# Seven half products per up-projection pair in the last feed-forward phase, and modulation weights two tiles at a time

## The chip, the core and the metric

The kernel runs on one core of a Trainium2 chip, in one launch. The metric is device time in microseconds (us): the median of three runs, beside which one execution was profiled.

## What is computed

Two layers of a decoder trunk for two request groups with the same weights: a prompt of 512 positions and 8 samples of 4 positions, 544 columns in all. Each layer is feed-forward, mixer (latent attention and a state-space branch), feed-forward; each of the three reads a normalised input that is scaled and shifted by a modulation made from a conditioning vector. What matters here:

```python
mod = (jax.nn.silu(c) @ ada_w + ada_b)[:, None, :]          # 1024 -> 9 * 1024
sh1, sc1, g1, shm, scm, gm, sh2, sc2, g2 = jnp.split(mod, 9, axis=-1)
...
h = rms_norm(x, norm_ffn2) * (1.0 + sc2) + sh2
a, b = jnp.split(h @ ffn2_up, 2, axis=-1)                   # 1024 -> 2 * 2816
x = x + 0.5 * g2 * ((jax.nn.silu(a) * b) @ ffn2_down)       # 2816 -> 1024
```

## The kernel before, in words

Activations lie transposed: features on the 128 partitions, the 544 columns in two halves of 272 (`HN`). Every float32 operand is split into a rounded part and a remainder (`hi`, `lo`), and every product of a weight tile with an input tile is three matmuls into one PSUM bank (`mm3`, lines 78 to 80): hi by hi, hi by lo, lo by hi. A weight unit of up to 128x1024 is loaded by SyncE's queue into one of five `raw` buffers (L55), copied to `whi` by ScalarE (L62) and subtracted to `wlo` by VectorE or GpSimd in turn (L65); `whl` has eight tiles, so four units.

`ffn` (one call per layer and half, four in all) goes through 22 pairs of up-projection tiles, `up[m]` and `up[22 + m]`. Each pair is 2 tiles x 8 k x 2 halves x 3 matmuls; `close_gate` then forms silu(a) * b and its `hi` and `lo` in the tile `mid[m]` (L327 to L331). Pairs 0 and 1 run together, column half 0 first (`front`), because the normalised input of half 1 (`norm_h`, L265 to L275) is still being made. When eight `mid` tiles are full, `do_down` multiplies a chunk of 6 or 8 of them with the down weights for all 8 output tiles and adds the result to `x` (`resid`, L290 to L295). The last chunk of the last phase is followed by the norm and the scaling of the output (`close`, `rstd`, `final`, L1488).

Beside this TensorE makes the modulations of later stages: `ada_steps` are 16 generators of which `tick()` advances the first one in the list by a step, at fixed places in the loops. A step is one weight tile of 128x1024 (k = 0 to 7): a load, and four matmuls of 32 stationary columns on strips of 32 rows of one PSUM tile (L153, two instructions each). They run in the first three phases; the last one has none. In the phases of layer 0 half 0 and layer 1 half 0 they are woven with the tables of the state-space branch (`s5_tables`).

The kernel is written in a tile framework: the order of each engine's instructions is set by a scheduler from the order of the code, from dependencies and from free buffers; buffers are given out as tiles are released. Each engine then takes its instructions strictly in that order.

Of the kernel before, what the change touches and what calls it, by code (L numbers as in the profile page):

```python
# [15 lines left out]
P = 128  # L16
D = 1024
# [8 lines left out]
FCH = ((0, 6), (6, 14), (14, 22))  # L26
NMID = 8
# [4 lines left out]
class Net:  # L32
# [113 lines left out]
    def ada_steps(self, l, i):  # L146
# [168 lines left out]
    def ffn(self, l, j, up, down, pool, spill=None):  # L315
        g = self.mod[l, 3 * j + 2] if (l, 3 * j + 2) in self.mod else None
        nc = self.nc
        mid = {}

# [36 lines left out]
        def do_up(ms):  # L356
            ms = list(ms)
            while ms:
                n = 2 if ms[0] == 0 else 1
                ws = []  # L360
                for m in ms[:n]:
                    self.share = l + j > 0 or m >= 8
                    ws.append((self.unit(up[m], D), self.unit(up[NFF + m], D)))
                    mid[m] = pool.tile([P, 2, 2, HN], F32R, tag="mid", name="mid")
                s = start(ws) if self.head else None
                for hf in range(2):
                    if n == 2:
                        def between():
                            if hf:
                                self.tick()  # L370
                            return self.settle()
                        pss = next(s) if s else self.front([u for w in ws for u in w], hf, between)
                        for i in range(n):
# [1287 lines left out]
```

## Time and profile before

| what | value |
|---|---|
| runs | 3056.64, 3065.47, 3057.44 us; median 3057.44 |
| profiled execution | 3048.91 us, its span 3047.1 us |
| mean granted TensorE clock | 0.98 of full speed |
| TensorE matmuls busy | 2888.8 us, 95% |
| VectorE, ScalarE, GpSimd busy | 1578.5, 878.6, 1236.9 us |
| HBM read and written | 452.99 and 61.75 MB |

The runs and the profiled execution are separate executions. "Busy" is the union of instruction times on an engine; TensorE's matmuls overlap (each is shown with 0.29 us, and the next starts 0.13 us after it), so rates are read from starts. A lower-case name such as `ps` or `mid` is a tile; L78 is line 78 of the kernel before.

### The profile page before, as it was taken

Reading aid. Unit: us, or ns where it says so; the run is one execution under the profiler, and the core shown is the slowest. Engines: PE = TensorE matmul, PEld = TensorE weight load, DVE = VectorE, ACT = ScalarE, POOL = GpSimd, SP = SyncE. Lnnn points to the kernel's source line nnn. Section 1 sums busy time; section 2 is a strip of 40 time slices with the busy share of each in tenths; the row PEclk is TensorE's granted clock in tenths of the full one; section 3 lists DMA queues with packets and bytes.
Section 4 is the critical chain, followed back from the end, with each engine's and each line's share of the span. In section 5 each row is a group of like instructions: output and inputs, shape, how many; then the busy total and the mean of one; then the engine's idle time right before and its main releaser. Section 6 shows DMA issues by size and latency. Waiting matters only on the chain.

```text
span 3047.1 us, 61485 instructions
## 1 busy us (share of the span) xinstructions
PE 2888.8 (95%) x24466; PEld 2677.5 (88%) x24466; DVE 1578.5 (52%) x3139; ACT 878.6 (29%) x1652; POOL 1236.9 (41%) x1434
## 2 busy tenths in 40 slices
PE   6999999999888999999999999999999899899998
PEld 5889999999667889989989999999987579899998
DVE  7384346374664464573454443464556534644344
ACT  3112123234342232122232222233344322322222
POOL 8635434481445249711233552236514551312113
PEclk9999999999999999999999999999999999999999
DMA  7596563647658624683225664345575774223221
GB/s 274 180 314 208 166 188 111 208 132 250 207 173 261 216 80 157 208 299 111 91 97 175 184 175 125 99 129 171 173 239 185 228 245 165 76 79 97 90 84 51
DMA packets 285008, 510.37 MB, mean 167 GB/s; under 512 B 73265, under 2 KB 166834, under 8 KB 284722
## 3 DMA queue, kind: packets, MB, share of 16 engines
q1 hardware_dynamic: 261746, 455.52, 47.2%
q0 software_dynamic: 13760, 42.03, 4.4%
q10 hardware_dynamic: 9216, 8.92, 0.9%
q8 instruction: 192, 3.15, 0.4%
q14 instruction: 94, 0.77, 0.1%
HBM read 452.99 MB, written 61.75 MB: 169 GB/s over the span
## 4 chain that ended last, share of the span: by engine, by line
PE 75%; DVE 8%; POOL 7%; issue 5%; DMA 3%; ACT 1%; SPq 0%; another core or an unknown queue 0%; DVEq 0%; ACTq 0%; POOLq 0%
PE ps L78 21%; PE ps L80 20%; PE ps L79 20%; PE ps L153 2%; PE ps L1264 2%; PE ps L1304 1%; PE ps L1136 1%; DVE ht L272 1%; DVE hlo L275 1%; PE ps L1176 1%; PE ps L786 1%; POOL s5a L729 1%; PE ps L785 1%; POOL s5b L730 1%; POOL s5a L731 1%
## 5 line engine op out<-in xcount | busy, mean ns | idle before, releaser
L78 PE MATMUL ps<-hhi,whi 128*128 128x272 f32 x3776 | 1105.9, 296 | 4.4 <-ACT whi L62 2.2
L79 PE MATMUL ps<-hlo,whi 128*128 128x272 f32 x3776 | 1092.8, 290 | 14.4 <-DVE hlo L275 11.7
L80 PE MATMUL ps<-hhi,wlo 128*128 128x272 f32 x3776 | 1096.1, 291 | 2.9 <-POOL wlo L65 1.8
L78 PEld LDWEIGHTS ps<-hhi,whi 128*128 128x128 f32 x3776 | 712.9, 190 | 54.7 <-issue 31.4
L79 PEld LDWEIGHTS ps<-hlo,whi 128*128 128x128 f32 x3776 | 718.1, 190 | 19.4 <-DVE hlo L275 13.4
L80 PEld LDWEIGHTS ps<-hhi,wlo 128*128 128x128 f32 x3776 | 715.9, 190 | 5.1 <-POOL wlo L65 2.1
L62 ACT CAST whi<-raw 128x1024 fp32r<-128x1024 f32 (+1 forms) x400 | 409.7, 1026 | 959.9 <-PE ps L79 584.4
L65 POOL TENSOR_TENSOR wlo<-raw,whi 128x1024 fp32r<-128x1024 f32 (+1 forms) x140 | 332.1, 2372 | 847.5 <-ACT whi L62 839.0
L65 DVE TENSOR_TENSOR wlo<-raw,whi 128x1024 fp32r<-128x1024 f32 (+1 forms) x260 | 322.8, 1242 | 354.7 <-ACT whi L62 332.0
L78 PE MATMUL ps<-mid,whi 128*128 128x272 f32 x1408 | 411.1, 292 | 2.6 <-ACT whi L62 2.6
L80 PE MATMUL ps<-mid,wlo 128*128 128x272 f32 x1408 | 407.0, 289 | 1.0 <-DVE wlo L65 1.0
L79 PE MATMUL ps<-mid,whi 128*128 128x272 f32 x1408 | 405.3, 288 | 0.0
L78 PEld LDWEIGHTS ps<-mid,whi 128*128 128x128 f32 x1408 | 265.1, 188 | 14.1 <-issue 9.9
L80 PEld LDWEIGHTS ps<-mid,wlo 128*128 128x128 f32 x1408 | 265.4, 188 | 1.5 <-DVE wlo L65 1.5
L79 PEld LDWEIGHTS ps<-mid,whi 128*128 128x128 f32 x1408 | 266.0, 189 | 0.2
L331 DVE TENSOR_TENSOR mid<-th,mid 128x272 fp32r<-128x272 f32 x176 | 192.9, 1097 | 88.9 <-ACT mid L330 88.3
L1351 POOL DMA_INDIRECT strm<-in_cacheT,idx x128 | 132.8, 1038 | 176.5 <-PE ps L1268 76.8
L1351 POOL DMA_INDIRECT strm<-in_cache,idx x128 | 128.7, 1006 | 133.2 <-PE ps L1304 77.3
L329 DVE TENSOR_TENSOR th<-th,ps 128x272 f32<-128x272 f32 x176 | 76.6, 436 | 203.1 <-PE ps L80 202.2
L292 DVE SCALAR_TENSOR_TENSOR x<-ps,mod,x 128x272 f32<-128x272 f32 (+1 forms) x224 | 106.7, 478 | 138.4 <-PE ps L80 138.2
L330 ACT CAST mid<-th 128x272 fp32r<-128x272 f32 x176 | 73.1, 416 | 318.9 <-DVE th L329 318.7
L78 PE MATMUL ps<-zhi,whi 128*128 128x272 f32 x512 | 153.2, 299 | 1.4 <-issue 1.2
(356 smaller groups left out, 4263.7 us busy)
## 6 DMA issues: line engine op xcount, KB each, us to landing
raw<-in_up SPq DMA_DIRECT2D x176, 512.0 KB
raw<-in_ada_w SPq DMA_DIRECT2D x144, 512.0 KB
raw<-in_dn SPq DMA_DIRECT2D x64, 512.0 KB
raw<-in_w_in SPq DMA_DIRECT2D x60, 512.0 KB
strm<-in_cacheT SPq DMA_DIRECT2D x128, 160.0 KB
s5WW<-w2scr SPq DMA_DIRECT2D x32, 512.0 KB
raw<-in_w_glu SPq DMA_DIRECT2D x32, 512.0 KB
strm<-in_cache SPq DMA_DIRECT2D x128, 128.0 KB
```

The costliest lines, as they stand in the source:

```text
L62: nc.scalar.copy(hi[:, :n], r[:, :n])
L65: e.tensor_sub(lo[:, :n], r[:, :n], hi[:, :n].bitcast(F32))
L78: nc.tensor.matmul(out, wh[:, s], rh, start=first, stop=False)
L79: nc.tensor.matmul(out, wh[:, s], rl, start=False, stop=False)
L80: nc.tensor.matmul(out, wl[:, s], rh, start=False, stop=last)
L153: nc.tensor.matmul(ps[32 * j:32 * j + 32, :256], self.cs[:, k], r[:, 256 * j:256 * j + 256], start=k == 0, stop=k == KD - 1)
L292: nc.vector.scalar_tensor_tensor(xx, ps[:, :np_], g[:, m, 0:1], xx, ALU.mult, ALU.add)
L329: nc.vector.tensor_mul(th, th, pb[:, :HN])
L330: nc.scalar.copy(mt[:, hf, 0], th)
L331: nc.vector.tensor_sub(mt[:, hf, 1], th, mt[:, hf, 0].bitcast(F32))
L1264: nc.tensor.matmul(po[32 * j:32 * j + 32], ql[:, a, 4 * bg + j].rearrange("p h t -> p (h t)"), X[j][:, P * a:P * a + P], start=a == 0, sto ...
L1351: self.nc.gpsimd.indirect_dma_start(out=out, out_offset=None, in_=src.rearrange("l n p f -> (l n p) f"), in_offset=bass.IndirectOffsetOnAx ...
```

## The change

In the last feed-forward phase (layer 1, second half) pairs 3 to 21 use Strassen's scheme on a 2x2 grid: two up-projection tiles, two halves of k (512 each), two column halves. `halves` loads both tiles and forms three combined weight tiles and a half one from them (A itself, S, B, S4), with subtractions on VectorE and GpSimd. `crossed` forms four combinations of the input's quarters (t3 and t2 during the front of half 1, t1 before pair 2, t4 after it); t4 takes over the place of a quarter that is no longer needed. `seven` issues seven products of 4 k x 3 matmuls, which share three PSUM banks; ScalarE copies partial sums out between them, and the sixth and seventh product of a pair (`ends`) are issued between the first three of the next pair, or within the next down chunk. To make room, this phase has six `mid` tiles, and its down projection is cut into five chunks of 4, 4, 4, 4 and 6 instead of 6, 8, 8.

In all phases a modulation step now loads two weight tiles in one tick and multiplies both in the next. `s5_setup` was divided into a loop over parts with one part, which does the same work.

```diff
 NFF = 22
-FCH = ((0, 6), (6, 14), (14, 22))
-NMID = 8
+FCH = (((0, 6), (6, 14), (14, 22)), ((0, 4), (4, 8), (8, 12), (12, 16), (16, 22)))
+NMID = (8, 6)
...
+    def halves(self, wa, wb):
+        nc = self.nc
+        V, E = nc.vector, nc.gpsimd
+        ra, rb = self.raw(wa, D), self.raw(wb, D)
+        lo, hi = slice(0, HK), slice(HK, D)
+        s = self.sum.tile([P, D], F32, tag="sum", name="sum")
+        A = self.split(ra, D, V)
+        V.tensor_add(s[:, hi], rb[:, lo], rb[:, hi])
+        V.tensor_sub(s[:, lo], s[:, hi], ra[:, lo])
+        E.tensor_sub(rb[:, lo], ra[:, lo], rb[:, lo])
+        S = self.split(s, D, V)
+        E.tensor_sub(ra[:, hi], ra[:, hi], s[:, lo])
+        B = self.split(rb, D, V)
+        h = self.sum.tile([P, HK], F32R, tag="s4h", name="s4h")
+        l = self.sum.tile([P, HK], F32R, tag="s4l", name="s4l")
+        nc.scalar.copy(h, ra[:, hi])
+        nc.vector.tensor_sub(l, ra[:, hi], h.bitcast(F32))
+        return A, S, B, (h, l)
+    def crossed(self, pool):
+        nc, V = self.nc, self.nc.vector
+        b11, b12, b21, b22 = self.h[0, 0], self.h[1, 0], self.h[0, 1], self.h[1, 1]
+        new = lambda pl, tag: tuple(pl.tile([P, 4, HN], F32R, tag=tag, name="hx") for _ in range(2))
+        t3, t2, t1 = (new(pool, "hx") for _ in range(3))
+        d = self.tmp.tile([P, 4, HN], F32, tag="ht", name="hd", bufs=1)
+        def add(x, b, i):
+            V.tensor_add(x, x, b[i][:, ks].bitcast(F32))
+        def sub(x, a, b, i):
+            V.tensor_sub(x, a[i][:, ks].bitcast(F32), b[i][:, ks].bitcast(F32))
+        def parts(t, x, ks):
+            nc.scalar.copy(t[0][:, ks], x)
+            V.tensor_sub(t[1][:, ks], x, t[0][:, ks].bitcast(F32))
+        pairs = [slice(0, 2), slice(2, 4)]
+        for ks in pairs:
+            x = d[:, ks]
+            sub(x, b22, b12, 0)
+            add(x, b22, 1)
+            V.tensor_sub(x, x, b12[1][:, ks].bitcast(F32))
+            parts(t3, x, ks)
+        for ks in pairs:
+            x = d[:, ks]
+            add(x, b11, 0)
+            add(x, b11, 1)
+            parts(t2, x, ks)
+        yield
+        def differ(t, a, b):
+            d = self.tmp.tile([P, 4, HN], F32, tag="ht", name="hd", bufs=1)
+            for k in pairs:
+                x = d[:, k]
+                V.tensor_sub(x, a[0][:, k].bitcast(F32), b[0][:, k].bitcast(F32))
+                V.tensor_add(x, x, a[1][:, k].bitcast(F32))
+                V.tensor_sub(x, x, b[1][:, k].bitcast(F32))
+                parts(t, x, k)
+        differ(t1, b12, b11)
+        yield
+        t4 = new(self.hp, "h")
+        differ(t4, b21, t2)
+        self.hx = t1, t2, t3, t4
+    def prod(self, ps, w, c0, rhs, first):
+        for k in range(4):
+            self.mm3(ps[:, :HN], w, c0 + k * P, P, (rhs[0][:, k], rhs[1][:, k]), first and k == 0, k == 3,
+                     skip_group_check=True)
...
         ps = self.psum()
-        for k in range(KD):
-            r = self.raw(self.t["ada_w"][l, k * P:(k + 1) * P, i * D:(i + 1) * D], D)
-            for j in range(4):
-                nc.tensor.matmul(ps[32 * j:32 * j + 32, :256], self.cs[:, k], r[:, 256 * j:256 * j + 256],
-                                 start=k == 0, stop=k == KD - 1)
-            if k < KD - 1:
+        for k0 in range(0, KD, 2):
+            rs = [self.raw(self.t["ada_w"][l, k * P:(k + 1) * P, i * D:(i + 1) * D], D) for k in (k0, k0 + 1)]
+            yield
+            for k, r in zip((k0, k0 + 1), rs):
+                for j in range(4):
+                    nc.tensor.matmul(ps[32 * j:32 * j + 32, :256], self.cs[:, k], r[:, 256 * j:256 * j + 256],
+                                     start=k == 0, stop=k == KD - 1)
+            if k0 < KD - 2:
                 yield
...
         def close_gate(pa, pb, mt, hf):
+            close_silu(open_silu(pa), pb, mt, hf)
+        def open_silu(pa):
             th = self.tmp.tile([P, HN], F32, tag="th", name="th")
             nc.scalar.activation(th, pa[:, :HN], AF.Tanh, scale=0.5)
             nc.vector.scalar_tensor_tensor(th, th, 1.0, pa[:, :HN], ALU.add, ALU.mult)
+            return th
+        def close_silu(th, pb, mt, hf):
             nc.vector.tensor_mul(th, th, pb[:, :HN])
             nc.scalar.copy(mt[:, hf, 0], th)
             nc.vector.tensor_sub(mt[:, hf, 1], th, mt[:, hf, 0].bitcast(F32))
+        def seven(m, mt):
+            A, S, B, S4 = self.halves(up[m], up[NFF + m])
+            t1, t2, t3, t4 = self.hx
+            V = nc.vector
+            new = lambda tag, **k: self.tmp.tile([P, HN], F32, tag=tag, name="u" + tag, **k)
+            X, Y, Z = (self.psum() for _ in range(3))
+            x, y, z = (p[:, :HN] for p in (X, Y, Z))
+            self.prod(Y, A, 0, self.h[0, 0], True)
+            p1 = new("sq")
+            nc.scalar.copy(p1, y)
+            end(0)
+            self.prod(Y, S, 0, t2, False)
+            q = new(("rr", "na")[m % 2], bufs=1)
+            nc.scalar.copy(q, y)
+            end(1)
+            self.prod(X, A, HK, self.h[0, 1], True)
+            V.tensor_add(p1, x, p1)
+            th = open_silu(p1)
+            self.tick()
+            self.prod(Y, B, 0, t3, False)
+            r = new(("acc0", "acc1")[m % 2], bufs=1)
+            nc.scalar.copy(r, y)
+            self.prod(Z, S, HK, t1, True)
+            V.tensor_add(r, z, r)
+            def third():
+                self.prod(Y, B, HK, t4, False)
+                close_silu(th, Y, mt, 0)
+                self.tick()
+            def fourth():
+                self.prod(Z, S4, 0, self.h[1, 1], False)
+                V.tensor_add(q, z, q)
+                close_silu(open_silu(q), r, mt, 1)
+                self.tick()
+            self.ends = [third, fourth]
+        def end(i):
+            if self.ends:
+                self.ends[i]()
+                if i:
+                    self.ends = None
 
...
                     self.share = l + j > 0 or m >= 8
+                    if m > 2 and cross:
+                        mid[m] = pool.tile([P, 2, 2, HN], F32R, tag="mid", name="mid")
+                        seven(m, mid[m])
+                        continue
                     ws.append((self.unit(up[m], D), self.unit(up[NFF + m], D)))
...
-                        pss = next(s) if s else self.front([u for w in ws for u in w], hf, between)
-                        for i in range(n):
-                            close_gate(pss[2 * i], pss[2 * i + 1], mid[i], hf)
-                        self.tick(2 + hf)
+                if ms[0] == 2 and cross:
+                    next(more)
+                for hf in range(2 if ws else 0):
+                    if n == 1:
+                        gate(ws[0], mid[ms[0]], hf)
+                        self.tick(hf)
+                        if hf and ms[0] == 2 and cross:
+                            next(more, None)
                         continue
-                    for m, w in zip(ms, ws):
-                        gate(w, mid[m], hf)
+                    def between():
                         if hf:
                             self.tick()
+                        return self.settle()
+                    pss = next(s) if s else self.front([u for w in ws for u in w], hf, between)
+                    if hf and cross:
+                        more = self.crossed(hx)
+                        next(more)
+                    for i in range(n):
+                        close_gate(pss[2 * i], pss[2 * i + 1], mid[i], hf)
+                    self.tick(2 + hf)
                 ms = ms[n:]
...
+            for i in range(2 if last else 0):
+                end(i)
             for m in range(KD):
                 ws[m] = self.unit(down[m][:, m0 * P:m1 * P], n * P)
                 one(m, 0)
+                if m == 0:
+                    for i in range(2):
+                        end(i)
                 if m < late:
                     one(m, 1)
...
-                     tc.tile_pool(name=f"ft{l}{half}", bufs=1, reuse_waits="tile") as ft:
+                self.ends = None
+                room = lambda c, name, bufs: c.enter_context(
+                    tc.tile_pool(name=f"{name}{l}{half}", bufs=bufs, reuse_waits="tile"))
+                with ExitStack() as rooms:
+                    cross = l * half
+                    pool, hx = room(rooms, "fm", NMID[cross]), None
+                    if cross:
+                        hx, self.sum = room(rooms, "fx", 6), room(rooms, "fs", 1)
+                    ft = room(rooms, "ft", 1)
                     self.share = True
...
-                        self.ffn(l, 2, t["up2"][l], t["dn2"][l], pool)
+                        self.ffn(l, 2, t["up2"][l], t["dn2"][l], pool, hx)
```

## Rows read from the trace of the kernel before

**Rows 1.** The page: its first line and the busy time of each engine.
```profile
span 3047.1 us, 61485 instructions
...
PE 2888.8 (95%) x24466; PEld 2677.5 (88%) x24466; DVE 1578.5 (52%) x3139; ACT 878.6 (29%) x1652; POOL 1236.9 (41%) x1434
```

**Rows 2.** Stretches: length, busy us (count) by engine, granted clock, DMA share, GB/s.
```profile
2670.00:2718.40 48.40, 48.40 (x386) 48.40 (x385) 22.49 (x29) 13.72 (x25) 9.75 (x5) 1.00 0.26 76
...
1700.00:1750.00 50.00, 50.00 (x429) 44.86 (x422) 27.52 (x50) 10.43 (x14) 27.10 (x29) 1.00 0.59 180
...
1300.00:1350.00 50.00, 47.38 (x377) 40.95 (x378) 37.58 (x67) 12.17 (x21) 7.97 (x3) 0.95 0.95 318
```

**Rows 3.** Timeline, VectorE in the last phase: start us, us, instruction, [idle before].
```profile
2682.17 2.42 DVE L331 TENSOR_TENSOR mid<-th,mid 128x272 fp32r<-128x272 f32 x1 [0.88 <-ACT mid L330]
...
2690.89 1.23 DVE L65 TENSOR_TENSOR wlo<-raw,whi 128x1024 fp32r<-128x1024 f32 x1 [2.61 <-ACT whi L62]
2692.03 0.43 DVE L328 SCALAR_TENSOR_TENSOR th<-th,ps 128x272 f32<-128x272 f32 x1
...
2694.27 2.42 DVE L331 TENSOR_TENSOR mid<-th,mid 128x272 fp32r<-128x272 f32 x1 [0.88 <-ACT mid L330]
...
2758.73 0.50 DVE L292 SCALAR_TENSOR_TENSOR x<-ps,mod,x 128x272 f32<-128x272 f32 x1 [1.61 <-PE ps L80]
```

**Rows 4.** Timeline, GpSimd in the same phase.
```profile
2681.90 2.39 POOL L65 TENSOR_TENSOR wlo<-raw,whi 128x1024 fp32r<-128x1024 f32 x1 [9.72 <-ACT whi L62]
...
2757.51 2.39 POOL L65 TENSOR_TENSOR wlo<-raw,whi 128x1024 fp32r<-128x1024 f32 x1 [7.45 <-ACT whi L62]
```

**Rows 5.** Instructions by line: count, ns min/median/max, first and last start, form.
```profile
L658 DVE TENSOR_TENSOR tX<-tF,tB x32: 676/692/2583, 145.9 to 1356.7; 128x512 f32<-128x512 f32 x32
...
L666 POOL TENSOR_TENSOR tW<-tS,tC x32: 1166/1172/1635, 150.1 to 1802.8; 128x576 f32<-128x576 f32 x32
...
L62 ACT CAST whi<-raw x8: 834/1048/1052, 2677.7 to 2717.1; 128x1024 fp32r<-128x1024 f32 x6, 128x768 fp32r<-128x768 f32 x2
...
L327 ACT ACTIVATE th<-ps x36: 383/391/400, 2655.2 to 2944.8; 128x272 f32<-128x272 f32 x36
```

**Rows 6.** Timeline, VectorE and GpSimd at the start of the last phase.
```profile
2648.31 0.29 DVE L269 TENSOR_TENSOR hlo<-ht,hhi 128x128 fp32r<-128x128 f32 x1
2655.31 1.23 DVE L65 TENSOR_TENSOR wlo<-raw,whi 128x1024 fp32r<-128x1024 f32 x1 [6.72 <-ACT whi L62]
...
2656.87 5.76 POOL L65 TENSOR_TENSOR wlo<-raw,whi 128x1024 fp32r<-128x1024 f32 x2 [27.53 <-ACT whi L62]
```

**Rows 7.** Timeline, VectorE in the tail.
```profile
3019.51 0.50 DVE L292 SCALAR_TENSOR_TENSOR x<-ps,mod,x 128x272 f32<-128x272 f32 x1 [2.52 <-PE ps L80]
...
3027.42 4.15 DVE L1488 SCALAR_TENSOR_TENSOR fo<-x,c_fing,ny 128x272 f32<-128x272 f32 x8
...
3032.06 0.18 DVE L290 TENSOR_TENSOR rs<-ps,mod 128x32 f32<-128x32 f32 x1
```

**Rows 8.** Timeline, TensorE around modulation steps.
```profile
55.16 0.64 PE L153 MATMUL ps<-raw,cs 128*32 128x256 f32 x8
...
1140.95 1.50 PE L153 MATMUL ps<-raw,cs 128*32 128x256 f32 x22
1142.38 0.76 PE L78 MATMUL ps<-hhi,whi 128*128 128x272 f32 x4
...
1678.61 0.29 PE L80 MATMUL ps<-hhi,wlo 128*128 128x272 f32 x1
1678.83 0.64 PE L153 MATMUL ps<-raw,cs 128*32 128x256 f32 x8
1679.39 0.39 PE L78 MATMUL ps<-hhi,whi 128*128 128x272 f32 x1
1679.62 0.29 PE L79 MATMUL ps<-hlo,whi 128*128 128x272 f32 x1
...
1784.27 0.64 PE L153 MATMUL ps<-raw,cs 128*32 128x256 f32 x8
```

More of the change, by code (lines that the diff above doesn't have):

```diff
@@ L74, in mm3 @@
+    def prod(self, ps, w, c0, rhs, first):
+        for k in range(4):
+            self.mm3(ps[:, :HN], w, c0 + k * P, P, (rhs[0][:, k], rhs[1][:, k]), first and k == 0, k == 3,
+                     skip_group_check=True)
+    def mm3(self, out, w, c0, m, rhs, first, last, **more):
         nc = self.nc
@@ L77, in mm3 @@
         s = slice(c0, c0 + m)
-        nc.tensor.matmul(out, wh[:, s], rh, start=first, stop=False)
-        nc.tensor.matmul(out, wh[:, s], rl, start=False, stop=False)
-        nc.tensor.matmul(out, wl[:, s], rh, start=False, stop=last)
+        nc.tensor.matmul(out, wh[:, s], rh, start=first, stop=False, **more)
+        nc.tensor.matmul(out, wh[:, s], rl, start=False, stop=False, **more)
+        nc.tensor.matmul(out, wl[:, s], rh, start=False, stop=last, **more)
     def setup(self):
@@ L318, in ffn @@
         mid = {}
+        cross = hx is not None
+        chunks, room = FCH[cross], NMID[cross]
         def gate(w, mt, hf):
@@ L365, in do_up @@
                 s = start(ws) if self.head else None
[L366 to L371, printed above, removed]
[L372 to L375 removed]
+                if ms[0] == 2 and cross:
[6 more added lines that the diff above has]
+                            next(more, None)
                         continue
[L377 to L378 removed]
+                    def between():
                         if hf:
                             self.tick()
+                        return self.settle()
[6 more added lines that the diff above has]
+                    self.tick(2 + hf)
                 ms = ms[n:]
         def do_down(c, last):
[L384 removed]
+            m0, m1 = chunks[c]
             n = m1 - m0
@@ L409, in ffn @@
         while done < NFF:
-            n = min(NMID - live, NFF - done)
+            n = min(room - live, NFF - done)
             do_up(range(done, done + n))
             done, live = done + n, live + n
-            if c < len(FCH) - 1 and done >= FCH[c][1] and (live == NMID or done == NFF):
+            if c < len(chunks) - 1 and done >= chunks[c][1] and (live == room or done == NFF):
                 do_down(c, None)
-                live -= FCH[c][1] - FCH[c][0]
+                live -= chunks[c][1] - chunks[c][0]
                 c += 1
@@ L458, in norm_tail, with s5_setup, s5_powers @@
             self.nc.sync.dma_start(out=spill[:, m, c], in_=self.x[:, m, c])
-    def s5_setup(self, l, pool):
+    def s5_setup(self, l, pool, parts=((0, 2),)):
+        for part in parts:
+            yield from self.s5_powers(l, pool, *part)
+    def s5_powers(self, l, pool, c0, c1):
         nc, t = self.nc, self.t
@@ L471, in s5_setup @@
         are, aim, dt = new("are"), new("aim"), new("dt")
-        nc.gpsimd.dma_start(out=are, in_=t["s5_re"][:, l])
-        nc.gpsimd.dma_start(out=aim, in_=t["s5_im"][:, l])
-        nc.gpsimd.dma_start(out=dt, in_=t["s5_dt"][:, l])
+        nc.gpsimd.dma_start(out=are, in_=t["s5_re"][:, l, cols])
+        nc.gpsimd.dma_start(out=aim, in_=t["s5_im"][:, l, cols])
+        nc.gpsimd.dma_start(out=dt, in_=t["s5_dt"][:, l, cols])
         MAGIC = 12582912.0
@@ L578, in s5_setup @@
         yield
-        for h in range(2):
+        for h in range(2 if c1 == 2 else 0):
             fp = pool.tile([P, 4, 2, N], F32, tag="s5fp", name="s5fp", bufs=1)
-            cmul(fp[0:N], pw[0:N, 4 * h:4 * h + 4, :, N:W], f[0:N, :, N:W], 4, N, N)
+            cmul(fp[0:N], pw[0:N, 4 * h:4 * h + 4, :, W - N:W], f[0:N, :, W - N:W], 4, N, N)
             nc.gpsimd.dma_start(out=self.fscr[l][4 * h:4 * h + 4].rearrange("n g q -> g n q"),
@@ L1527, in run @@
                 self.fillers, todo = todo[:n], todo[n:]
-                with tc.tile_pool(name=f"fm{l}{half}", bufs=NMID, reuse_waits="tile") as pool, \
-                     tc.tile_pool(name=f"ft{l}{half}", bufs=1, reuse_waits="tile") as ft:
+                self.ends = None
[7 more added lines that the diff above has]
+                    ft = room(rooms, "ft", 1)
                     self.share = True
```

12 lines of the change are left out of this document (7 added, 5 removed).

## The prediction

> **What bounds the kernel now.** I read the page's table of engines first, then stretches, then single instructions. TensorE is busy 2888.8 of a span of 3047.1 us and nothing else comes near [rows 1]. A share says little of one stage, so the next view is busy time by stretch: in an up-projection stretch of the last feed-forward phase TensorE is busy 48.40 of 48.40 us at full clock, VectorE 22.49, ScalarE 13.72, GpSimd 9.75, and DMA takes 0.26; the modulation steps of the earlier phases run beside an equally full TensorE (50.00 of 50.00), but in a stretch like 1300 to 1350 DMA stands at 0.95 and TensorE at 47.38 [rows 2]. So TensorE's instruction stream sets the time at both places of the change, and a matmul taken out is worth its slot as long as the helpers keep up. How near are they? In one pair's period VectorE runs a weight split of 1.23 us, two gates of 0.43 to 0.44 us operations, and one `mid` subtraction that takes 2.42 us although it is no longer than its sisters [rows 3]. It starts at 2682.17, and GpSimd's split runs 2681.90 to 2684.29 [rows 4]: a VectorE operation with two SBUF operands stands until GpSimd's is done. One with an operand in PSUM doesn't: L292 at 2758.73 takes its usual 0.50 us [rows 3] inside GpSimd's 2757.51 to 2759.90 [rows 4]. This decides the forecast.
>
> **Seven products instead of eight: TensorE.** A pair now is 2 tiles x 8 k x 2 halves x 3 = 96 matmuls, and the pairs come every 2694.27 - 2682.17 = 12.10 us [rows 3], so 0.126 us a matmul. Seven products of 4 x 3 are 84, or 10.59 us. Pairs 3 to 21, 19 of them, save 1.51 us each: **-28.7 us**. The down projections keep their 1056 matmuls. Their cut into five chunks adds 16 smaller weight units and 32 more evacuations; a four-tile unit gives TensorE 24 x 0.126 = 3.0 us, while VectorE needs two or three operations of 0.50 us or less per product and a half-size split, under 2.2 us together. I cost that at nothing; the cover is gone only if VectorE enters the chunk late.
>
> **The pair's helpers.** VectorE gets per pair: three splits of 1.23 (3.69), three half-width operations at the 0.69 of a 512-column one (2.07) [rows 5], and nine of 272 columns at 0.44 (two mid subtractions, three additions, four gate steps; 3.96): 9.7 us. Back to back an operation costs 0.09 less (1.14 from 2690.89 to 2692.03 for one of 1.23 [rows 3]): 8.4. GpSimd does two 512-column subtractions; 576 columns take 1.17 [rows 5] and half of 2.39 [rows 4] is 1.20, so 2.4 us, and 11 of VectorE's 15 operations have both inputs in SBUF and stand meanwhile. VectorE's demand is thus between 8.4 and 9.7 + 2.4 = 12.1 us against TensorE's 10.59: from below it to level with today's pair. I take the middle with the lock mostly felt, 10.9, which costs 0.3 x 19 = **+6 us** (ends 0 and 1.5 x 19 = 28.7). ScalarE needs three casts of 1.05, half a one, and seven of 0.39 to 0.42, 6.5 us, so it is covered, but the second product writes the bank whose first result it copies: it has one product (12 x 0.126 = 1.5 us) for a copy near 0.39 [rows 5] that may queue behind a cast.
>
> [...]
>
> **The crossed sums at the start.** Before the first such pair VectorE forms four combinations of the input: 30 operations of 544 columns, at 0.69 x 544/512 = 0.73, or 0.65 back to back. Fourteen (9.1 us) can start when the last `hlo` ends at 2648.6 and last to 2657.7. Today VectorE starts pair 2's split at 2655.31, with GpSimd on the next two from 2656.87 [rows 6]. Now four gate operations (1.4) and that split (1.2) come behind the sums, to 2660.3 at best, against 2656.5: 3.8 us, and part of GpSimd's 2.4 on top, say 5. The other sixteen (10.4 us), pair 2's gates and pair 3's halves must fit in pair 2's 12.1 us and pair 3's first products; I find VectorE 2 to 3 us late there. Together **+8 us** (3 if the scheduler fits them in, 14 if nothing more than half of 30 x 0.73 = 21.9 is hidden; below nothing is excluded, since no old work leaves this stretch).
>
> **The tail.** After the half-0 result of the last m (its VectorE step follows at 3019.51) TensorE has four products of eight tiles, 3.0 us each, and VectorE fills that time with the norm and the eight final scalings of half 0, 3027.42 to 3031.6; the last residual starts at 3032.06 [rows 7]. With six tiles they take 2.3 us each: 3 us less cover, of which only the earlier norm sum gives 0.7 back: **+2 us** (0 to 3).
>
> **Modulation steps, two tiles at a time.** The loads are the same and come a tick earlier than the matmuls; the count of ticks stays 8. What changes is how often TensorE leaves the 128x128 work for four strips of 32 columns. From L80 at 1678.61 to L79 at 1679.62 is 1.01 us with one step between, where two slots are 0.25: 0.76 us a step, and from the step's start to the next matmul 0.56. Eleven matmuls in a row (22 instructions, three rounds over the strips) take 1.43 [rows 8]: a further round adds (1.43 - 0.56)/2 = 0.43. Two steps together cost 0.76 + 0.43 = 1.19 instead of 1.52: 0.33 a merger. Between 55.16 and 1784.27 I count 111 stretches of one step [rows 8] and 6 longer ones besides the opening one, 118 in all, for 128 steps; in pairs there are at most 64, so 54 fewer: 18 us. Some ten mergers lie where DMA is the limit [rows 2] and give little: **-15 us** (ends 0, if the scheduler pulls the two steps apart, and -18).
> [...]
> Held against this: two of the five `raw` buffers wait for a tick, so weights are fetched less far ahead. A 512 KB unit feeds TensorE for 6 us and the split tiles hold two pairs, so I cost it at nothing; without that cover each late unit would cost its landing.
>
> **Sum.** -28.7 + 6 + 8 + 2 - 15 = -28 us. The profiled execution took 3048.9 us (its span and 1.8 around it), 8.5 below the median of the runs, 3057.4. So 3021 profiled and **3029 us** in the runs. What a measurement of this kernel can tell from no change is about 0.3%, 9 us.
>
> **Rivals.**
> - *All hidden.* VectorE stays under TensorE (8.4 us a pair), the sums cost 3: -28.7 + 3 + 2 - 18 = -42, 3015 us. For it: VectorE was busy under half the time [rows 2], and down chunks let it catch up. Against: the 2.42 us wait. Chance 0.17.
> - *The pairs of steps don't run together.* If TensorE takes up other work between them: -13, 3045 us. For it: the order is the scheduler's; against: both loads land long before. Chance 0.10.
> - *VectorE level with today's pair.* 12.1 us a pair: +8 + 2 - 15 = -5, 3052 us, which is no change. For it: the lock, and a queue that is taken in order. Against: four of the operations read PSUM. Chance 0.13.
> - *Slower: VectorE becomes the bound.* To 12.1 us comes a wait in VectorE's queue for ScalarE's cast of 1.05 us ahead of a split, because one operation that waits holds all behind it: 13.2, +1.1 x 19 = 21, +8 + 2 - 15 = +16, 3073 us. It decides from a pair time of 12.1 + (9 + 5)/19 = 12.8 us. For it: every sum of halves is a chain over VectorE, GpSimd and ScalarE; against: it runs a pair ahead. Chance 0.07.
> - *Forecast*, -15 to -41 about 3029: chance 0.53.
>
> Faster: 0.53 + 0.17 + 0.10 = 0.80; within 0.3%: 0.13; slower: 0.07. The range leaves out the slower case, half of the level one and the far end of the first: 3010 to 3052. The forecast's own is 3016 to 3042.
>
> **What would show it.** Per step: pairs 3 to 21 some 10.9 us apart instead of 12.10, with TensorE's waits on VectorE or ScalarE; near 12 the lock has won. GpSimd's 512-column subtractions near 1.2 us, and VectorE operations stretched over them. A TensorE gap of some 5 us before pair 2, and another in pair 3 or 4. Modulation stretches of 16 instructions, some 0.98 us to the next matmul, half as many as now. A last residual some 2 us later against the end of half 0. It would be wrong if VectorE waits for ScalarE inside the pair, if the split tiles (six of eight used by one pair) make ScalarE wait past the next pair's start, or if late weights open gaps in the earlier phases.

## Result, and the profile after

The changed kernel took 3015.09 us (median of four runs, 3012.52 to 3017.05), the kernel before 3057.04 beside it: ratio 0.9861, interval [0.984, 0.9882], 42 us faster. 3029 had been predicted, with 3010 to 3052 as the range.

The profiled executions differ by less, 3047.1 against 3013.2 us of span (-33.9), because the one of before lay 8.1 us under the median beside it and the one of after at its median. The mixers, which the change doesn't touch, were also 5.4 us longer in the profile of after; outside them the span falls by 39.3 us, from 1869.3 to 1830.0. The page of the changed kernel, its first line and TensorE's:

```profile
span 3013.2 us, 61535 instructions
...
PE 2847.7 (95%) x24238; PEld 2657.3 (88%) x24238; DVE 1705.2 (57%) x3393; ACT 940.3 (31%) x1771; POOL 1254.7 (42%) x1461
```

Beside [rows 1], VectorE has 127 us more to do and TensorE 41 less; TensorE's share of the span stays at 95%. Where that comes from is read by stretch (length, busy us and count of each engine, granted clock, DMA share, GB/s):

```profile
140.00:160.00 20.00, 7.49 (x50) 6.37 (x49) 14.37 (x15) 2.48 (x5) 13.93 (x14) 0.69 0.79 245
...
1700.00:1750.00 50.00, 50.00 (x436) 46.02 (x436) 22.87 (x45) 11.55 (x16) 23.74 (x25) 1.00 0.62 194
...
2650.00:2700.00 50.00, 47.29 (x373) 46.80 (x373) 48.42 (x79) 24.62 (x47) 13.16 (x8) 1.00 0.27 78
...
2700.00:2767.00 67.00, 67.00 (x535) 67.00 (x534) 53.34 (x98) 30.51 (x54) 17.88 (x12) 1.00 0.32 97
```

The last row is one cycle of the new last phase, four pairs and a down chunk: TensorE never stands, and VectorE has 13.7 us to spare. At the phase's start (2650 to 2700) VectorE is full and TensorE loses 2.7 us. At 140 us, far from the products, TensorE is busy 7.49 of 20 us at 0.69 of its clock, where the kernel before has

```profile
140.00:160.00 20.00, 15.27 (x109) 13.11 (x108) 9.64 (x14) 1.20 (x4) 9.53 (x11) 0.83 0.83 248
```

This is the other side of the change, below. TensorE's timeline of the changed kernel (start, duration, instruction, [idle before <- what ended it]):

```profile
151.51 0.59 PE L154 MATMUL ps<-hhi,whi 128*128 128x272 f32 x1 [8.62 <-ACT whi L63]
...
156.23 0.60 PE L156 MATMUL ps<-hhi,wlo 128*128 128x272 f32 x1 [3.90 <-DVE wlo L66]
...
1671.14 1.07 PE L231 MATMUL ps<-raw,cs 128*32 128x256 f32 x16
1672.14 0.39 PE L154 MATMUL ps<-hhi,whi 128*128 128x272 f32 x1
...
2621.51 0.70 PE L325 MATMUL ps<-lsq,ones 128*128 128x272 f32 x2 [2.83 <-DVE lsq L324]
...
2646.70 0.39 PE L154 MATMUL ps<-hhi,whi 128*128 128x272 f32 x1 [0.99 <-ACT whi L63]
...
2665.12 0.39 PE L154 MATMUL ps<-hx,whi 128*128 128x272 f32 x1 [1.78 <-ACT hx L111]
...
2676.12 0.39 PE L156 MATMUL ps<-hx,wlo 128*128 128x272 f32 x1 [0.92 <-DVE wlo L66]
...
2742.87 0.29 PE L154 MATMUL ps<-hhi,s4h 128*128 128x272 f32 x1
...
2753.45 0.29 PE L154 MATMUL ps<-hhi,s4h 128*128 128x272 f32 x1
...
3000.47 0.73 PE L325 MATMUL ps<-lsq,ones 128*128 128x272 f32 x2 [4.36 <-DVE lsq L324]
```

The product with `s4h` comes once a pair, but in three of its four places in a cycle the next one is nearer or farther, because the scheduler moves it against the other products and the down chunk. The two shown have 84 matmuls between them, all of products, and are 2753.45 - 2742.87 = 10.58 us apart, with no wait. The same product of the next cycle starts 66.40 us later (2733.81 to 2800.21) for 4 x 84 + 192 = 528 matmuls, 0.126 us each, so nothing is added in the rest of the cycle either. A stretch of two steps has 16 instructions and takes 1.00 us; with the opening one there are 67 stretches instead of 120, 53 fewer. From the norm's sum at 2621.51 to the end the last phase takes 391.7 us, 23.5 less than before. The first and the last sum of that phase in the kernel before:

```profile
2631.89 0.70 PE L247 MATMUL ps<-lsq,ones 128*128 128x272 f32 x2 [2.83 <-DVE lsq L246]
...
3034.10 0.73 PE L247 MATMUL ps<-lsq,ones 128*128 128x272 f32 x2 [2.11 <-DVE lsq L246]
```

Stage lengths from the profiles of all kernels follow (us, each from the last sum of squares ahead of a stage to the first one behind it, the last phase to the end of the span). The experiments were made in three series (B, C, D), each on one chip and beside runs of the kernel before; series B has the kernel before as a profile of its own.

| kernel | first ffn, layer 0 | second ffn, layer 0 | first ffn, layer 1 | mixers | last phase |
|---|---|---|---|---|---|
| before | 481.1 | 429.4 | 420.0 | 588.9, 588.9 | 415.2 |
| after | 476.1 | 422.7 | 415.9 | 595.0, 588.2 | 391.7 |
| B: e0_before | 479.5 | 430.7 | 420.0 | 551.3, 553.0 | 415.3 |
| B: e1_products | 481.5 | 432.1 | 419.9 | 553.7, 551.4 | 392.5 |
| B: e2_steps | 478.2 | 430.4 | 415.9 | 551.2, 554.5 | 413.5 |
| B: e6_chunks | 483.0 | 431.8 | 419.9 | 553.6, 550.9 | 416.1 |
| C: e10_after | 478.0 | 427.2 | 415.8 | 596.4, 593.5 | 394.1 |
| C: e11_raw6 | 473.0 | 418.8 | 415.8 | 594.0, 596.8 | 391.8 |
| C: e12_steps_raw6 | 473.2 | 419.9 | 415.8 | 593.8, 598.1 | 415.2 |
| C: e7_no_sums | 476.6 | 423.1 | 415.8 | 595.2, 590.6 | 388.6 |
| D: e3_no_gpsimd | 477.3 | 426.1 | 415.8 | 587.7, 587.8 | 389.8 |
| D: e4_vector3 | 474.8 | 424.8 | 415.7 | 593.2, 588.1 | 395.2 |
| D: e5_vector6 | 476.6 | 424.6 | 415.7 | 594.0, 589.3 | 424.3 |
| D: e15_raw6_no_gpsimd | 474.8 | 424.4 | 415.8 | 594.3, 592.0 | 390.5 |

A part of the scatter in the last column is TensorE's clock: over the first 30 us of the phase 0.89 of it is granted in e10_after, e11_raw6 and e15, 0.94 in before, e0_before, after, e1_products, e3 and e7, 1.00 in e2_steps and e6_chunks. A difference of 0.05 to 0.06 over 30 us is 1.5 to 1.8 us.

### The profile page after: what moved, and what is told of

The parts are those of the page before. It is cut to its first block, busy times and chain, and to the rows that moved or that the text cites. A ratio compares the mean times of both kernels' runs of the same rounds, so it can differ in the third digit from the quotient of the medians.

```text
span 3013.2 us, 61535 instructions
## 1 busy us (share of the span) xinstructions
PE 2847.7 (95%) x24238; PEld 2657.3 (88%) x24238; DVE 1705.2 (57%) x3393; ACT 940.3 (31%) x1771; POOL 1254.7 (42%) x1461
## 4 chain that ended last, share of the span: by engine, by line
PE 74%; DVE 9%; POOL 7%; issue 4%; DMA 3%; ACT 1%; another core or an unknown queue 1%; SPq 0%; DVEq 0%; ACTq 0%; POOLq 0%
PE ps L154 21%; PE ps L156 20%; PE ps L155 20%; PE ps L1290 1%; PE ps L231 1%; PE ps L1418 1%; PE ps L1458 1%; PE ps L1330 1%; DVE ht L350 1%; POOL s5a L883 1%; PE ps L940 1%; PE ps L939 1%; DMA raw<-in_dn 1%; DVE hlo L353 1%; DMA raw<-in_up 1%
## 5 line engine op out<-in xcount | busy, mean ns | idle before, releaser
L154 PE MATMUL ps<-hhi,whi 128*128 128x272 f32 x3320 | 969.9, 296 | 14.4 <-ACT whi L63 11.8
L155 PE MATMUL ps<-hlo,whi 128*128 128x272 f32 x3320 | 962.5, 291 | 14.4 <-DVE hlo L353 11.7
L156 PE MATMUL ps<-hhi,wlo 128*128 128x272 f32 x3320 | 963.7, 292 | 7.1 <-DVE wlo L66 4.1
L63 ACT CAST whi<-raw 128x1024 fp32r<-128x1024 f32 (+2 forms) x416 | 412.9, 994 | 904.3 <-PE ps L155 443.9
L154 PEld LDWEIGHTS ps<-hhi,whi 128*128 128x128 f32 x3320 | 627.4, 190 | 47.4 <-issue 21.6
L155 PEld LDWEIGHTS ps<-hlo,whi 128*128 128x128 f32 x3320 | 633.4, 191 | 19.2 <-DVE hlo L353 13.2
L156 PEld LDWEIGHTS ps<-hhi,wlo 128*128 128x128 f32 x3320 | 630.4, 190 | 10.1 <-DVE wlo L66 5.1
L66 POOL TENSOR_TENSOR wlo<-raw,whi 128x1024 fp32r<-128x1024 f32 (+2 forms) x129 | 290.6, 2253 | 671.7 <-ACT whi L63 603.7
L66 DVE TENSOR_TENSOR wlo<-raw,whi 128x1024 fp32r<-128x1024 f32 (+2 forms) x287 | 358.4, 1249 | 338.2 <-ACT whi L63 316.2
L370 DVE SCALAR_TENSOR_TENSOR x<-ps,mod,x 128x272 f32<-128x272 f32 (+1 forms) x256 | 121.6, 477 | 106.5 <-PE ps L156 106.3
L155 PE MATMUL ps<-zlo,whi 128*128 128x272 f32 x512 | 149.1, 291 | 2.8 <-issue 2.6
```

Of the source, the lines that this page charges most:

```text
L63: nc.scalar.copy(hi[:, :n], r[:, :n])
L66: e.tensor_sub(lo[:, :n], r[:, :n], hi[:, :n].bitcast(F32))
L154: nc.tensor.matmul(out, wh[:, s], rh, start=first, stop=False, **more)
L155: nc.tensor.matmul(out, wh[:, s], rl, start=False, stop=False, **more)
L156: nc.tensor.matmul(out, wl[:, s], rh, start=False, stop=last, **more)
L370: nc.vector.scalar_tensor_tensor(xx, ps[:, :np_], g[:, m, 0:1], xx, ALU.mult, ALU.add)
```

## The experiments

**The two halves of the change, each alone.** A copy of the kernel before says what the comparison can tell; the other kernels have the products with the old steps, the steps without the products, and the smaller chunks without either.

> The kernel before once more, to see how far two executions and two profiles of the same program differ. The change brought 42 us in the medians of the runs but only 33.9 us between the two profiled spans (3047.1 and 3013.2), and the mixer of layer 0 looked 6.1 us longer after. If the first profile of before was merely a quick execution: ratio 1.000 within 0.3%, a profiled execution near 3056 us, and the missing 8 us spread over the two mixers, which the change does not touch. If the spans are typical instead, a profiled execution near 3049 again, and the 8 us is something that the change does when it is not profiled.

Measured: 2975.49 us, ratio 1.0001 [0.9988, 1.0014]. The profiled execution took 2975.26, the median of its runs. The chip is another one, on which the same kernel takes 82 us less, so this doesn't say whether the first profile of before was a quick one. But outside the mixers the two spans agree, 1869.2 us here and 1869.3 there.

e1_products keeps `ada_steps` of before in the changed kernel:

```diff
-        for k0 in range(0, KD, 2):
-            rs = [self.raw(..., D) for k in (k0, k0 + 1)]
+        for k in range(KD):
+            r = self.raw(self.t["ada_w"][l, k * P:(k + 1) * P, i * D:(i + 1) * D], D)
...
```

> The seven products alone, with modulation steps of one tile as before. Theory now: the helpers are nearly hidden, and the last phase gains 12 x 19 x 0.126 = 28.7 us less 3 us of waits at its start and 2 us in the tail, so 23 to 24 us: 3033 us where before takes 3057, ratio 0.992. Rival, the sum of the forecast: the helpers cost 16 us, so 13 us gained, 3044 us, ratio 0.996, and the steps must then bring 29 us.

Measured: 2954.81, ratio 0.9931 [0.9916, 0.9945], -20.4 us. Its last phase is 22.8 us shorter than that of the copy.

e2_steps is the reverse edit, made to the kernel before.

> The modulation steps in pairs alone, in the kernel before. Theory: 53 stretches of steps fewer at 0.33 us are 17 us, less some lost to loads near 150 us: 3040 to 3042 us, ratio 0.995. Rival: the steps bring 25 us or more (3032 us or less), because a load that comes a tick earlier also takes waits out of TensorE. Rival: they bring under 8 us, and the remainder of the 42 us came with the products.

Measured: 2965.68, ratio 0.9966 [0.9954, 0.9978], -9.6 us in the medians (10 by the ratio). The phase in which TensorE hardly waits for anything else (first of layer 1, 0.5 us of waits) gave 420.0 - 415.9 = 4.1 us for 12 fewer stretches, 0.34 a merger, against 0.33 forecast. The first phase gave only 1.3 against the copy, though it loses the most stretches (24 of 53). The four kernels with single steps take 479.5 to 483.0 us there, so one pair of profiles says little; but its timeline shows waits for weights that the copy doesn't have,

```profile
152.08 0.60 PE L78 MATMUL ps<-hhi,whi 128*128 128x272 f32 x1 [8.62 <-ACT whi L62]
...
156.64 0.59 PE L80 MATMUL ps<-hhi,wlo 128*128 128x272 f32 x1 [3.75 <-DVE wlo L65]
```

the same two as in the changed kernel. The copy has four smaller ones near there: between 120 and 180 us TensorE waits 12.4 us here and 7.8 in the copy. Its waits in the whole phase are 24.0 us against 17.6 in the copy, and 11.9 against 9.2 in the second.

e6_chunks cuts the down projection of the last phase into five, in the kernel before:

```diff
-FCH = ((0, 6), (6, 14), (14, 22))
-NMID = 8
+FCH = (((0, 6), (6, 14), (14, 22)), ((0, 4), (4, 8), (8, 12), (12, 16), (16, 22)))
+NMID = (8, 6)
```

> The kernel before with six mid tiles and five down chunks (4, 4, 4, 4, 6) in the last phase, without the products. Theory: the matmuls are the same and the 16 further units and 32 evacuations are hidden, so only the tail counts: with six tiles in the last chunk 3 us less of TensorE's work covers the norm and scaling of half 0, of which 0.7 to 1 comes back: +2 us, 3059 us, ratio 1.0007. Rival: every further chunk border costs TensorE a wait of its own, +1 to 3 us each, 3062 to 3066 us.

Measured: 2979.81, ratio 1.0017 [1.0006, 1.0029]. The wait before the last norm sum grows by 2.3, to that of the changed kernel, 4.36 us, where the copy waits 2.10 (TensorE's timeline of e6_chunks):

```profile
2965.11 1.28 PE L247 MATMUL ps<-lsq,ones 128*128 128x272 f32 x2 [4.36 <-DVE lsq L246]
```

So the tail's 2.3 us come from the chunks and their six tiles alone. The last phase is 416.1 us against 415.3, only 0.8 longer, because in its first 30 us the copy had the lower clock and got through 13 matmuls fewer, some 1.6 us (e0_before, then e6_chunks):

```profile
2558.23:2588.23 30.00, 27.75 (x199) 26.90 (x200) 20.89 (x47) 10.48 (x22) 4.99 (x2) 0.94 0.08 22
```

```profile
2562.34:2592.34 30.00, 27.75 (x212) 26.91 (x213) 22.31 (x48) 10.87 (x23) 5.76 (x2) 1.00 0.12 41
```

The runs differ by 4.6 us, with an interval from 1.8 to 8.6 that holds the tail's 2.3; where the rest lies stays open.

**The whole change again, and the raw buffers.** The waits at 152 us had one suspect: a pair of steps holds two of the five `raw` buffers for a tick. e11 and e12 give the pool a sixth.

```diff
-        self.rawp = pool("rawp", 5)
+        self.rawp = pool("rawp", 6)
```

> The whole change, on the same chip as the three kernels below. Alone, the products were worth 20.4 us and the paired steps 10.2 us of 2975 on one chip, while the whole change was worth 42 of 3057 on another. If the parts add up, the ratio is near 0.990 (some 30 us); if the first comparison holds wherever the kernel runs, 0.986 (some 41 us). The last feed-forward phase should be 391 to 393 us from its norm's sum to the end of the span, either way.

Measured: 3024.95 against 3059.89, ratio 0.9875 [0.9855, 0.9896], -35 us; the last phase is 394.1 us, 1 over what was expected. The product of the ratios of the two halves is 0.9897, at the upper edge of this interval and outside that of the first comparison, though it is itself uncertain by some 0.002. Whether the parts do a little more together, or gain a little more on these chips, is not settled.

> The whole change with six raw buffers instead of five. Theory: two of the five buffers held by a pair of steps make the weights late, and the sixth lets a load start earlier: TensorE's waits for a split near 152 to 157 us (8.6 and 3.8 us) and near 1260 us (7.5) shrink to 3 to 4 each, and the time is 6 to 10 us below that of the whole change. Rival: in those stretches the DMA engines are full, the bytes land no earlier, and the time is the same within 2 us.

Measured: 3018.37, ratio 0.9865 [0.9847, 0.9883]; 6.6 us below e10_after, with intervals that overlap. SyncE's queue shows what the buffer changes. First the changed kernel, then e11_raw6:

```profile
121.94 3.17 SPq L56 DMA_DIRECT2D raw<-in_ada_w  x2
125.21 1.25 SPq L56 DMA_DIRECT2D raw<-in_up  x1
140.69 0.65 SPq L782 DMA_DIRECT2D tF<-fscr  x1
...
145.26 0.38 SPq L56 DMA_DIRECT2D raw<-in_up  x1
```

```profile
121.17 1.28 SPq L56 DMA_DIRECT2D raw<-in_ada_w  x3
124.09 0.80 SPq L56 DMA_DIRECT2D raw<-in_up  x2
140.54 0.66 SPq L782 DMA_DIRECT2D tF<-fscr  x1
```

With five buffers one up-projection tile is left for 145.26, behind eight loads of tables in the same queue, the first of which waits 14.2 us for its source to be written; with six it goes out at 124.09 with its sister. TensorE in the same 20 us of e11_raw6:

```profile
140.00:160.00 20.00, 13.92 (x119) 12.04 (x118) 14.33 (x17) 2.16 (x5) 13.02 (x13) 0.91 0.80 259
```

13.92 us busy instead of 7.49, at a DMA share of 0.80 against 0.79: it was a late issue, and not full DMA engines, that held this weight. Not all of it comes back: e11_raw6 then waits 4.72 us at 157 (the next weights), and between 120 and 180 us 9.1 in all, where the changed kernel waits 12.5. The two phases of layer 0 are 473.0 and 418.8 us, against 474.8 to 478.0 and 422.7 to 427.2 in the six profiles of the paired steps with the products and five buffers.

> The kernel before with the paired steps alone and six raw buffers. With five, 10.2 us were gained of some 16 that the fewer stretches give. Theory of the held buffers: 15 to 18 us below the kernel before. Rival (DMA full): 10, as with five buffers.

Measured: 3045.40, ratio 0.9956 [0.9939, 0.9973], -14.5 us, near the theory's lower figure, but the interval (8 to 19 us) holds the rival's 10 as well: the runs alone don't decide here. The three phases with steps gained 7.9 + 9.5 + 4.2 = 21.6 us against the first profile of before. Its mixers are 14 us longer than there, but mixers of kernels that run the same paired steps go from 587.7 to 598.1, so a part of the gain is hidden in that scatter.

**The sums of the input.** Here `crossed` makes nothing, and plain quarters go into the products, so the up-projection is another one (the edit also removes the body of `crossed`):

```diff
...
-        differ(t4, b21, t2)
+        t1, t2, t3, t4 = b12, b11, b22, b21
         self.hx = t1, t2, t3, t4
```

> The whole change without the crossed sums of the input: plain quarters of the input stand in the place of the sums in four of the seven products, so the up-projection of the last phase is another one. It prices the sums: the forecast put them at 8 us (5 before the second pair, the rest in the third or fourth); the rival, that the scheduler fits most of them in, at 3. TensorE's waits ahead of the second to fourth pair (together some 4 us in the profile after) should vanish: 3 to 4 us below the whole change by the rival, 8 by the forecast.

Measured: 3017.79, ratio 0.986 [0.9835, 0.9884]. Its last phase is 388.6 us against 394.1, 391.7 and 391.8 in the three profiles with the sums (e10_after, after, e11_raw6), so they cost 3 to 5.5 us; the 3.1 against after are at the same clock in the first 30 us. Its stretch at the start has TensorE full and VectorE at 39.15:

```profile
2650.00:2700.00 50.00, 50.00 (x399) 50.00 (x398) 39.15 (x61) 23.55 (x45) 13.38 (x9) 1.00 0.31 94
```

**GpSimd beside VectorE, and VectorE's cover.** Three kernels: the two GpSimd subtractions given to VectorE, and three or six additions a pair that nobody needs.

```diff
-        V, E = nc.vector, nc.gpsimd
+        V, E = nc.vector, nc.vector
```

> The whole change with the pair's two GpSimd subtractions done by VectorE. VectorE gets 2 x 0.69 = 1.4 us more a pair and is no longer held up by GpSimd there. Theory (VectorE has cover, 53 to 54 us busy of 67 in a cycle of four pairs and a down chunk): the pairs stay 10.6 us apart and the last phase stays at 391 to 394 us. Rival, VectorE bounds the pair with the lock's cost on top (the forecast's 6 us): the last phase gets some 6 us shorter if the lock was dearer than the work, or up to 1.4 x 19 = 27 longer if the work is.

Measured: 3014.30, ratio 0.9865 [0.9847, 0.9882]; the last phase is 389.8 us. Groups by line of two cycles (2700 to 2833), busy us and mean ns, first of the changed kernel:

```profile
L66 DVE TENSOR_TENSOR wlo<-raw,whi 128x1024 fp32r<-128x1024 f32 x16 | 23.5, 1467 | 1.7 <-ACT whi L63 1.7
L66 DVE TENSOR_TENSOR wlo<-sum,whi 128x1024 fp32r<-128x1024 f32 x8 | 11.8, 1474 | 6.2 <-ACT whi L63 6.2
L84 DVE TENSOR_TENSOR sum<-sum,raw 128x512 f32<-128x512 f32 x8 | 9.3, 1166 | 0.1
...
L85 POOL TENSOR_TENSOR raw<-raw 128x512 f32<-128x512 f32 x8 | 13.7, 1706 | 29.1 <-DVE sum L83 17.9 <-DVE rs L368 6.8 <-PE ps L155 4.4
...
L87 POOL TENSOR_TENSOR raw<-raw,sum 128x512 f32<-128x512 f32 x8 | 10.6, 1329 | 34.6 <-DVE wlo L66 34.6
```

and of e3_no_gpsimd:

```profile
L66 DVE TENSOR_TENSOR wlo<-raw,whi 128x1024 fp32r<-128x1024 f32 x16 | 19.5, 1221 | 2.4 <-ACT whi L63 2.4
L66 DVE TENSOR_TENSOR wlo<-sum,whi 128x1024 fp32r<-128x1024 f32 x8 | 9.8, 1222 | 4.9 <-ACT whi L63 4.9
L85 DVE TENSOR_TENSOR raw<-raw 128x512 f32<-128x512 f32 x8 | 6.6, 821 | 0.0
L84 DVE TENSOR_TENSOR sum<-sum,raw 128x512 f32<-128x512 f32 x8 | 5.5, 686 | 0.1
L87 DVE TENSOR_TENSOR raw<-raw,sum 128x512 f32<-128x512 f32 x8 | 5.5, 684 | 0.1
```

Beside GpSimd's two subtractions the three splits of a pair take 0.25 us more on average (1467 and 1474 ns against 1221 and 1222) and `L84` 0.48 (1166 against 686): 1.2 us of VectorE's time a pair, out of the 3.0 us that GpSimd's two take. VectorE does them itself in 1.5. So VectorE is as busy either way (106.5 us of these 133 in after, 107.8 here), TensorE is full in both, and over the cycle this cost the path nothing.

At the phase's start it is different. The last phase is 1.9 us shorter than in after, with the same clock in its first 30 us, and of the waits at 2646.70, 2665.12 and 2676.12 in the changed kernel, 3.7 us together, one of 0.75 is left:

```profile
2643.38 0.39 PE L156 MATMUL ps<-hhi,wlo 128*128 128x272 f32 x1 [0.75 <-DVE wlo L66]
```

The kernel before has one of 0.74 in the same place, and so has e15 below, which also keeps GpSimd out of the pairs; with GpSimd these waits are 1.6 to 3.7 us (e11, e1, e10 and after). Two waits on the norm ahead of them are 1.1 longer in e3, which leaves the 1.9. So the price of the crossed sums is paid where GpSimd's subtractions come on top of them, while VectorE has no free time (48.42 of 50 us above). Whether because VectorE's operations get longer beside them or because GpSimd's 1.3 to 2.7 us stand in a pair's chain, these kernels don't separate.

For the dose, `halves` ends with

```diff
+        for _ in range(3):
+            more = self.sum.tile([P, HK], F32, tag="more", name="more")
+            V.tensor_add(more, s[:, lo], s[:, hi])
         return A, S, B, (h, l)
```

> The whole change with three more 512-column VectorE additions a pair, whose result nobody reads: 3 x 0.69 = 2.1 us a pair, 39 us in 19 pairs. VectorE's free time is some 13 us in a cycle of four pairs and a chunk, 3.3 a pair. Theory (free time of the whole cycle counts): hidden, the last phase 391 to 396 us. Rival (what counts is the pair alone, because TensorE can't run ahead of the splits): VectorE at 9.7 to 10.5 plus 2.1 is over 10.59 and the last phase is 20 to 39 us longer.

> As the one above with six additions: 4.1 us a pair. Theory (whole cycle): 0.8 us a pair more than VectorE's free time, the last phase 10 to 25 us longer. Rival (the pair alone): 59 to 78 us longer.

Measured: three additions, 3020.23, ratio 0.9887 [0.9861, 0.9912], last phase 395.2 us; six, 3050.15, ratio 0.9974 [0.9957, 0.999], last phase 424.3. The cycle in e4_vector3, then in e5_vector6:

```profile
2767.00:2834.00 67.00, 67.00 (x535) 67.00 (x534) 61.85 (x110) 30.43 (x53) 19.30 (x12) 1.00 0.31 96
```

```profile
2700.00:2767.00 67.00, 63.83 (x495) 63.10 (x495) 65.37 (x111) 26.80 (x47) 17.65 (x11) 0.98 0.30 95
```

The first three go into VectorE's free time (53 to 54 us busy become 62, TensorE stays full), at 1 to 4 us for the phase; the next three don't. The theory that the whole cycle's free time counts holds for the place of the bend. Its price for six was too low (10 to 25 us against 33). The trace says where the 33 lie: TensorE waits 28.0 us in the phase, 9.7 in after, and it is granted less of its clock, 0.95 against 0.98: behind its waits of 2.76 us (to 2697.72) and 3.31 us (to 2984.96) matmuls start 0.23 us apart for 4.0 and 3.3 us, where they otherwise start 0.126 apart. The whole phase of after, then of e5_vector6:

```profile
2621.51:3013.20 391.69, 369.93 (x2908) 367.84 (x2908) 316.82 (x580) 166.25 (x297) 106.39 (x77) 0.98 0.27 83
```

```profile
2623.76:3048.10 424.34, 384.01 (x2908) 377.53 (x2908) 393.55 (x694) 164.02 (x297) 118.46 (x77) 0.95 0.25 77
```

The waits are 18 us more, and the clock is worth some 13 by estimate: 0.05 of 424 us against 0.02 of 392.

**A version with both.** Six buffers and no GpSimd in the pair:

> A version that could beat both: the whole change with six raw buffers and without the two GpSimd subtractions. The sixth buffer alone gave 6.6 us in the runs and 13 in the profiled stretches of the first layer. If GpSimd's part is hidden either way, the ratio is that of six buffers alone, 0.985 to 0.988; if the lock costs something, some 0.002 lower.

Measured: 3006.44, ratio 0.9836 [0.982, 0.9852], the best of all kernels run; e3_no_gpsimd on the same chip has 0.9865 [0.9847, 0.9882], so the sixth buffer is worth some 8 us there, with intervals that overlap a little. Both up-projection tiles go out at 124.16 in its profile, as in e11_raw6, but its phases of layer 0 (474.8, 424.4) lie among those with five buffers: it was taken of the slowest of its five runs (3018.90). So the runs favour the sixth buffer three times out of three, by 5 to 8 us, each time with intervals that overlap.

## Why the prediction was right, and where its sizes were not

The direction held, TensorE's stream set the time as forecast, and the time lies in the range; but 3015 is the time of the rival *All hidden*, to which the forecast gave a chance of 0.17, and 1 us outside the forecast's own range. In the second comparison (-35 us) it would have lain within. Term by term:

- **Products, -28.7.** Right: 84 matmuls in 10.58 us, and 19 such pairs (76 matmuls `hhi,s4h`, four a pair). The last phase checks it: -28.7, +3.1 of TensorE's waits (5.38 us against 2.24 between the first and the last sum) and +2.3 in the tail make -23.3; -23.5 was measured, -22.8 in e1_products.
- **Helpers, +6.** This step failed: time that VectorE loses beside GpSimd was taken for a delay of TensorE. The demand was well sized, between 8.4 and 12.1 us a pair: a pair's operations take 11.3 us in the groups of the two cycles, 10 without their overlap. GpSimd's two take 3.0 us and not 2.4. What was left out is the cover that the forecast itself named for the rival: in the down chunk VectorE catches up, and 13 us a cycle are free, 3.3 a pair. e4_vector3 and e5_vector6 show the bend between 2.1 and 4.1 us more a pair. What the forecast calls the lock stands in the trace as a split of 2.11 us beside GpSimd's subtraction of 1.29, where the splits of e3_no_gpsimd take 1.22 (VectorE's timeline, then GpSimd's):

```profile
2716.22 2.11 DVE L66 TENSOR_TENSOR wlo<-raw,whi 128x1024 fp32r<-128x1024 f32 x1
```

```profile
2715.96 1.29 POOL L85 TENSOR_TENSOR raw<-raw 128x512 f32<-128x512 f32 x1 [3.39 <-DVE rs L368]
```

  Not every such subtraction costs VectorE its whole length: of 3.0 us a pair it is 1.2.
- **Crossed sums, +8.** Right in place, too dear: 3.1 us by TensorE's waits, 3 to 5.5 by e7_no_sums, and near nothing in e3_no_gpsimd, so it is at this place that GpSimd's part was felt. The gap of 5 us before pair 2 was 0.99. VectorE's timeline shows why:

```profile
2645.17 1.22 DVE L66 TENSOR_TENSOR wlo<-raw,whi 128x1024 fp32r<-128x1024 f32 x1
2646.31 0.43 DVE L411 SCALAR_TENSOR_TENSOR th<-th,ps 128x272 f32<-128x272 f32 x1
2646.66 0.72 DVE L105 TENSOR_TENSOR hd<-hd,hlo 128x544 f32<-128x544 f32 x1
2647.29 0.43 DVE L411 SCALAR_TENSOR_TENSOR th<-th,ps 128x272 f32<-128x272 f32 x1
2647.64 2.59 DVE L105 TENSOR_TENSOR hd<-hd,hlo 128x544 f32<-128x544 f32 x1
```

  Pair 2's split (2645.17) and two gates of pairs 0 and 1 (`L411`) stand among the last two sums (`L105`), and ahead of the two remainders that close the fourteen at 2654.08, where the forecast had put split and gates behind all fourteen. The bound of 3 us, "if the scheduler fits them in", was the right end.
- **Tail, +2.** Right in size: 4.36 us against 2.11 before the last sum, and e6_chunks gives the cause. Its sign of being right didn't come: the last residual starts 12.04 us after half 0's last step (2986.65 to 2998.69 in VectorE's timeline), not 2 us later than the 12.55 of before. VectorE's chain is about as long as it was; 24 matmuls fewer lie beside it, so TensorE waits.
- **Modulation steps, -15.** Right in sum, wrong in its parts. The first profile gained 5.0 + 6.7 + 4.1 = 15.8 us in the three phases; over the six profiles with products, pairs and five buffers the gains are 3.1 to 6.3, 2.2 to 6.7 and 4.1 to 4.3, in mean 13. Alone they gave 9.6 in the runs. The 0.33 us a merger is right where nothing else binds, 0.34. "I cost it at nothing" of the held `raw` buffers was wrong: the loads are behind table loads in SyncE's queue, and the tile that no longer fits in the pool waits for them. A sixth buffer gave 6.6 us beside the whole change, 4.9 beside the steps alone (14.5 against 9.6, on different chips). The count was near: 54 stretches fewer were forecast from 118, the trace has 53 fewer from 120.
- With the measured sizes (13 for the steps, their mean) the sum is -28.7 + 0 + 3 + 2 - 13 = -37, between the -35 and the -42 of the two comparisons.
- Of the rivals, VectorE as the bound needs over 2.1 us more a pair than this kernel has; the steps of a pair did run together (16 instructions in a row).

## What to carry to other kernels

Here a VectorE with more to do cost little until its free time over a whole cycle of the loop was gone (2.1 us more a pair cost 1 to 4 us in the phase, 4.1 us cost 33), and it cost time where there was none, as at the start of this phase (3 to 5.5 us for the sums): add a known dose of dead work to an engine and look for the bend, before paying to relieve it. A step that takes two loads at a time also takes two buffers at a time; the price is paid by the next load in the same queue, here 21 us later (145.26 against 124.09), so count what stands ahead of it there. And if a sum depends on where a scheduler puts new work, its likely value is nearer to the cheap end when there are gaps to fill.

## What the hardware showed that was not expected

The mixers, which the change doesn't touch, took 551 to 555 us each on the chip of series B, and 588 to 598 on the others. The first mixer as a whole in the changed kernel, then in e0_before:

```profile
515.32:1110.34 595.02, 557.08 (x5053) 500.58 (x5054) 314.17 (x731) 197.62 (x421) 236.84 (x328) 0.96 0.61 192
```

```profile
518.83:1070.14 551.31, 537.76 (x5054) 488.95 (x5054) 313.06 (x731) 198.01 (x421) 236.72 (x328) 0.99 0.65 207
```

The work is the same. On one chip TensorE is granted 0.96 of its clock and is busy 557 us, on the other 0.99 and 538; that is 19 of the 44 us. The other 24 are time in which TensorE stands (38 us against 14). The feed-forward phases, where TensorE hardly waits, agree within 2 us. Why the mixers differ by chip was not tried.

Around the waits for weights near 152 us the granted clock was lower, too. In the 20 us around the two waits of the changed kernel it is 0.69, and behind them, from 156.62 to 161.38, matmuls start 0.23 us apart (157.08, 157.30, 157.53) instead of 0.126. In e11_raw6, with the shorter waits, the same stretch has 0.91; but there too its wait of 4.72 us is followed by 0.50 from 157 to 162. Over 130 to 180 us the two kernels are granted 0.86 and 0.90.
